# The pool layer of a two-block network: seven-product projections, the residual through DRAM, and norms by half rows

## The chip, the cores and the metric

The kernel runs on one core of one Trainium2 chip. The metric is the device time of one execution in microseconds (us). Names used below: PE is TensorE (matmuls; PEld its weight loads), DVE is VectorE, ACT is ScalarE, POOL is GpSimd, SP is SyncE, which here only issues DMAs.

## What is computed

Two networks run one after the other on 1024 rows of 1024 features, in 32-bit floats. The first has two layers: windowed attention, then the pool layer that this case is about, then a norm. The second has one block (neighbourhood attention, a gated recurrence, a mix w_o, an MLP). Cut to the part that matters:

```python
def pool_layer(h, w_in, w_mix, scale, w_out):
    u, z = jnp.split(h @ w_in, [POOL_WIDTH], axis=-1)          # 1024 -> 2 x 1024
    p = multiscale_pool(u)                                     # windows 2, 4, 8, 16; one per group of 256
    m = jnp.einsum('bsgc,gcd->bsgd', p, w_mix).reshape(B, S, POOL_WIDTH) * scale
    return (m * jax.nn.silu(z)) @ w_out

x = x + attn_layer(rmsnorm(x, norm_g[0]), ...)
x = x + pool_layer(rmsnorm(x, norm_g[1]), ...)
x = rmsnorm(x, final_g)                                        # end of the first network
a = rms_norm(h, norm_mix)                                      # start of the second
```

`multiscale_pool` takes for each group the mean over the last 2, 4, 8 or 16 rows, less the row itself.

## The kernel before

**Precision.** Every operand of a large product is split into a high part (a rounded copy, made by ACT) and a low part (the difference, made by DVE or POOL). `mm3` issues three matmuls for each 128x128 by 128x512 term: high x high, low x high, high x low (lines 108, 110, 111). `split_w` (L79, L80) and `split_evac` (L118, L119) make the parts. Weights go through three buffers each for the raw tile (`wraw`) and its parts (`whi`, `wlo`).

**Order.** The program is written in order of the data; a scheduler places each engine's instructions by that order and by its own estimate of when inputs are ready. `issue_after(i)` keeps the instructions of a block behind instruction i on i's engine. All waits are made automatically, by the tile that is read or overwritten. A pool's memory can be taken again when the tiles that lay there are done with.

**End of attention.** The residual X of 8 row tiles sits in SBUF. The output projection runs over four pairs of k blocks (kp), each over two column halves and eight row tiles, and adds each bank to X (`out_piece`, L281). Four row tiles are normed (`norms`, into copies), turned by PE into the feature-major operand `xx` (`transposed`, L175 to L178), the other four after the first weights of the pool layer have run.

**Pool layer.** It loops over four groups g. In each, two column blocks of u are projected over both row halves (`pieces_fm`, evacuated by ACT at L620), pooled by DVE (window sums L632, difference L639, parts L118 and L119), then two blocks of z with SiLU (L653), then the mix product (evacuated at L662 with scale and z), and the result m times the group's 256 rows of w_out is added to X (`add_out`, L539). So the output projection is spread over the groups. In group 3 it runs in two row halves: behind each row tile a hook squares X (L683), multiplies by final_g (L686, six row tiles on POOL, two on DVE), stores the product to `d_h` and squares again; `group` forms the two norms of four row tiles at once, the scaled copies are turned (`feature_major`), and the first pieces of two gate projections (`gate0`, `gate1`) fill PE meanwhile.

**Where the other scheme is already used.** The second block computes three products by seven half-size products instead of eight (Strassen's scheme in Winograd's form): with the row halves and the k (or column) halves as 2x2 blocks, sums S1 to S4 of the blocks of the operand and sums of the weight blocks are made, and seven products are added into banks. For w_o this is a sequence of `times` over four banks each (L1391), with `split_a`, `split_b` and `less` (L1375, weight differences) between; for the up projection it is `first_two`, `sums` (L1634 to L1648) and `pair`, which handles two column blocks at a time: weight sums (`weight_sums`, by `vec`, L1595), products A11, A12, S2, S1, S3, S4, A22 of 12 matmuls each, evacuations by ACT (L1540) and adds by DVE (L1544); for the down projection blocks are stored to DRAM (`d_u`) and read back through a ring of three buffers, the residual through `d_x` (adds at L1791).

Of the kernel before, what the change touches and what calls it, by code (L numbers as in the profile page):

```python
# [30 lines left out]
def fused_kernel(tc, a, out, stop=None, dbg=None):  # L31
# [180 lines left out]

    x = a["x"][0]
# [17 lines left out]
    w_in = a["attn_w_in"][0]  # L231
    w_out = a["attn_w_out"][0]
    def norm_into_xt(gcol, alloc, pool, xtag="xn", xbufs=5):

        xx = XT()

        def norms(half):
            xn = []
            for i, n in ((0, 4),) if half == 0 else ((0, 2), (2, 2)):
                ss = small.tile([P, n], F32, name="nm" if n == 2 else "ss4")  # L240
                for j in range(n):
                    junk = pool.tile([P, 1024], BF16, name="junk", bufs=1)
                    nc.scalar.activation(out=junk, in_=X[:, half * 4 + i + j, :], func=AF.Square,
                                         accum_out=ss[:, j:j + 1])
                r = rsqrt(ss, D)
                for j in range(n):
                    xr = pool.tile([P, D], F32, name=xtag, bufs=xbufs)
                    if j % 2:
                        nc.scalar.activation(out=xr, in_=X[:, half * 4 + i + j, :], func=AF.Copy, scale=r[:, j:j + 1])
                    else:  # L250
                        nc.vector.tensor_scalar_mul(xr, X[:, half * 4 + i + j, :], r[:, j:j + 1])
                    xn.append(xr)
            return xn

        def do(half, xn=None):
            transposed(alloc, xn or norms(half), gcol, xx, half * 4)
        return xx, norms, do

# [24 lines left out]
    with lay:  # L283
# [213 lines left out]
        xpool = xp.enter_context(tc.tile_pool(name="xpool", bufs=1, side="right"))  # L497
        X = xpool.tile([P, NT, D], F32, name="X")
        up2 = xp.enter_context(tc.tile_pool(name="up2", bufs=1, side="right"))
        pst = xp.enter_context(tc.tile_pool(name="pst", bufs=4, space=PSUM))  # L500
        psm = xp.enter_context(tc.tile_pool(name="psm", bufs=4, space=PSUM))
        for t in range(NT):
            if t < 4:
                nc.gpsimd.tensor_copy(out=X[:, t, :512], in_=x0[:, t, :])
                nc.scalar.dma_start(out=X[:, t, 512:], in_=x[t * P:(t + 1) * P, 512:])
            else:
                nc.scalar.dma_start(out=X[:, t, :], in_=x[t * P:(t + 1) * P, :])
# [3 lines left out]
        xx, norms, norm_half = norm_into_xt(g_pool, lambda k: pst.tile([P, 512], F32, name="tp"), up2, "pp", 6)  # L511
        for kp in range(4):
            ws = {}
            if kp == 3:
                ws = {ch: out_weights(kp, ch) for ch in range(2)}
                wu0 = w_cols(a["pool_w_in"][0], 0)
            for ch, t in ([(ch, t) for ch in range(2) for t in range(NT)] if kp < 3 else
                          [(ch, t) for t in range(NT) for ch in range(2)]):
                if ch not in ws:
                    ws[ch] = ws0[kp] if kp < 2 and ch == 0 else out_weights(kp, ch)  # L520
                if kp >= 2 or ch or t >= 4:
                    out_piece(psm, kp, ws[ch], X[:, t, ch * 512:ch * 512 + 512], t)
                if kp == 3 and (ch, t) == (1, 5):
                    xn = norms(0)
                if kp == 3 and (ch, t) == (1, 6):
                    norm_half(0, xn)
    dump("x1", X)
# [4 lines left out]
    def add_out(ps_pool, terms, ws_by_ch, hook=None, scale=None, tiles=range(NT), half=None, by_ch=False):  # L532

        for t, ch in [(t, ch) for ch in range(2) for t in tiles] if by_ch else [(t, ch) for t in tiles for ch in range(2)]:
            csl = slice(ch * 512, ch * 512 + 512)
            ps = ps_pool.tile([P, 512], F32, name="mm")
            mm3(ps, list(zip(terms(t), ws_by_ch[ch])))
            if scale is None:
                nc.vector.tensor_tensor(out=X[:, t, csl], in0=X[:, t, csl], in1=ps, op=ALU.add)  # L539
            else:  # L540
                nc.vector.scalar_tensor_tensor(out=X[:, t, csl], in0=X[:, t, csl], scalar=scale[:, t:t + 1],
                                               in1=ps, op0=ALU.mult, op1=ALU.add)
            if half:
                half(t, ch)
            if hook and ch:
                hook(t)

    w2 = a["w_in_2"][0]
    dram = ctx.enter_context(tc.tile_pool(name="dram", bufs=1, space=bass.MemoryType.DRAM))
# [25 lines left out]
    with ExitStack() as ph:  # L575
# [35 lines left out]
        for g in range(4):  # L611
# [59 lines left out]
            if g < 3:  # L671
                add_out(psm, terms, mixed((0, 1)))
# [675 lines left out]
    def turned(half, k):  # L1348
# [3 lines left out]
        return ps  # L1352

# [510 lines left out]
```

## Time and profile before

| | us |
|---|---|
| median of 3 runs | 2377.55 (2375.57 to 2377.82) |
| profiled execution | 2379.98 |
| its span, first to last instruction | 2378.2 |
| PE busy | 2309.6 |
| DVE, ACT, POOL busy | 1426.5, 971.5, 791.5 |

The granted TensorE clock is 0.992 of full speed in the mean. Times inside the span count from its first instruction. The pool layer lies from about 461 to 780 us, the w_o product of the second block from 1636 to 1730, its up projection from 1730 to 2050, its down projection from there to the end.

### The profile page before, as it was taken

The page shows a single profiled execution, that of the slowest core. Times are in us where ns is not written, and L with a number is a line of the kernel's source. Part 1 is how long each engine was busy: PE and PEld are TensorE (multiplying, and loading weights), DVE is VectorE, ACT ScalarE, POOL GpSimd, SP SyncE. Part 2 cuts the span into 40 slices and gives each one's busy share as a digit, 9 for nine tenths or more (in the row PEclk, how much of TensorE's full clock was granted, in tenths as well). Part 3 has the DMA queues.
Part 4 walks back from the last instruction along what each step waited for, and adds up shares of the span by engine and source line. Part 5 has one row for each costly group of instructions (what it writes and reads, how often), then busy time and mean ns, then how long its engine had stood idle before and what let it go on. Part 6 is the DMA issues. An engine that isn't in the chain of part 4 may idle for free. (4 is left out here: it accounts for less than half of the span.)

```text
span 2378.2 us, 32052 instructions
## 1 busy us (share of the span) xinstructions
PE 2309.6 (97%) x12054; PEld 1921.4 (81%) x12054; DVE 1426.5 (60%) x2602; ACT 971.5 (41%) x1808; POOL 791.5 (33%) x528
## 2 busy tenths in 40 slices
PE   7999999999999999999999999999989999999997
PEld 6877777888887888878988888877768888878886
DVE  5566677654367255553265746759784444786775
ACT  5344452422226454543232232423555555533334
POOL 2112123112226343431212112126354444444455
PEclk9999999999999999999999999999999999999999
DMA  5111103111124222211111111467235444754331
GB/s 160 36 28 36 28 27 108 40 45 58 40 63 138 62 68 67 54 58 45 46 52 54 41 54 54 139 200 258 71 120 199 146 151 164 267 220 168 107 124 71
DMA packets 237147, 230.01 MB, mean 97 GB/s; under 512 B 59896, under 2 KB 179022, under 8 KB 233408
## 3 DMA queue, kind: packets, MB, share of 16 engines
q1 hardware_dynamic: 228176, 210.31, 27.5%
q10 hardware_dynamic: 8224, 16.00, 1.8%
q0 software_dynamic: 592, 1.65, 0.3%
q8 instruction: 95, 1.56, 0.3%
q14 instruction: 60, 0.49, 0.1%
HBM read 168.68 MB, written 59.24 MB: 96 GB/s over the span
## 5 line engine op out<-in xcount | busy, mean ns | idle before, releaser
L108 PE MATMUL mm<-xh,whi 128*128 128x512 f32 (+2 forms) x1744 | 670.9, 385 | 8.5 <-DVE st L1544 3.7
L110 PE MATMUL mm<-xl,whi 128*128 128x512 f32 (+2 forms) x1744 | 665.3, 382 | 0.0
L111 PE MATMUL mm<-xh,wlo 128*128 128x512 f32 (+2 forms) x1744 | 662.3, 380 | 2.3 <-POOL wlo L80 2.2
L80 POOL TENSOR_TENSOR wlo<-wraw,whi 128x1024 fp32r<-128x1024 f32 (+1 forms) x127 | 300.2, 2369 | 894.3 <-ACT whi L79 838.4
L108 PEld LDWEIGHTS mm<-xh,whi 128*128 128x128 f32 x1744 | 329.2, 189 | 70.2 <-issue 3.5
L111 PEld LDWEIGHTS mm<-xh,wlo 128*128 128x128 f32 x1744 | 329.3, 189 | 66.1 <-POOL wlo L80 3.4
L110 PEld LDWEIGHTS mm<-xl,whi 128*128 128x128 f32 x1744 | 329.4, 189 | 56.2
L79 ACT CAST whi<-wraw 128x1024 fp32r<-128x1024 f32 (+1 forms) x127 | 128.9, 1018 | 371.8 <-PE mm L110 174.3
L111 PE MATMUL mm<-whi,xl 128*128 128x512 f32 (+1 forms) x688 | 247.8, 360 | 0.0
L110 PE MATMUL mm<-wlo,xh 128*128 128x512 f32 (+1 forms) x528 | 184.6, 350 | 3.3 <-POOL wlo L119 2.6
L108 PE MATMUL mm<-whi,xh 128*128 128x512 f32 (+1 forms) x528 | 184.7, 350 | 2.1 <-DVE X L281 1.3
L111 PEld LDWEIGHTS mm<-whi,xl 128*128 128x128 f32 x688 | 130.7, 190 | 19.3
L108 PE MATMUL mm<-whi,xl 128*128 128x512 f32 x352 | 138.5, 394 | 4.7 <-ACT whi L118 2.4
L110 PE MATMUL mm<-wlo,xl 128*128 128x512 f32 x352 | 138.8, 394 | 3.9 <-POOL wlo L119 3.9
L1668 POOL TENSOR_TENSOR wlo<-raw,whi 128x1024 fp32r<-128x1024 f32 (+1 forms) x42 | 84.1, 2003 | 100.8 <-ACT whi L1667 100.8
L110 PEld LDWEIGHTS mm<-wlo,xh 128*128 128x128 f32 x528 | 99.8, 189 | 17.2 <-POOL wlo L119 3.9
L108 PEld LDWEIGHTS mm<-whi,xh 128*128 128x128 f32 x528 | 99.8, 189 | 15.4 <-DVE X L281 1.7
L119 POOL TENSOR_TENSOR wlo<-wraw,whi 128x1024 fp32r<-128x1024 f32 x30 | 80.6, 2692 | 80.4 <-ACT whi L118 78.0
L1595 DVE TENSOR_TENSOR st<-st 128x512 f32<-128x512 f32 x64 | 61.1, 975 | 57.8 <-ACT st L1581 56.8
L1791 DVE TENSOR_TENSOR X<-X,mm 128x512 f32<-128x512 f32 x112 | 73.1, 680 | 37.2 <-PE mm L111 37.2
L878 DVE CUSTOM_DVE_ANT_0 s<-S,bi 128x400 f32<-128x400 f32 x64 | 34.5, 571 | 94.6 <-PE S L870 94.6
L119 DVE TENSOR_TENSOR pl<-PT,ph 100x512 fp32r<-100x512 f32 (+2 forms) x128 | 83.6, 668 | 10.3 <-ACT ph L118 9.3
(370 smaller groups left out, 4400.1 us busy)
## 6 DMA issues: line engine op xcount, KB each, us to landing
wraw<-in_w_in_dram SPq DMA_DIRECT2D x48, 512.0 KB, 3.8
d_S<-st SPq DMA_DIRECT2D x64, 256.0 KB, 4.7
raw<-in_w_up_dram SPq DMA_DIRECT2D x30, 512.0 KB, 5.0
d_A<-st ACTq DMA_DIRECT2D x48, 256.0 KB, 2.0
fa<-d_S SPq DMA_DIRECT2D x10, 1024.0 KB, 4.9
wraw<-in_pool_w_in_dram SPq DMA_DIRECT2D x18, 512.0 KB, 3.9
fa<-d_A SPq DMA_DIRECT2D x9, 1024.0 KB, 4.8
wraw<-in_attn_w_in_dram SPq DMA_DIRECT2D x32, 256.0 KB, 3.2
```

The lines of the kernel that those rows point to most:

```text
L79: nc.scalar.copy(out=hv[:, i:i + n], in_=view[:, i:i + n])
L80: nc.gpsimd.tensor_tensor(out=lv[:, i:i + n], in0=view[:, i:i + n], in1=f(hv[:, i:i + n]), op=ALU.subtract)
L108: nc.tensor.matmul(ps, lhsT=lh[0], rhs=rh[0], start=first and i == 0, stop=False, skip_group_check=chain)
L110: nc.tensor.matmul(ps, lhsT=lh[0], rhs=rh[1], start=False, stop=False, skip_group_check=chain)
L111: nc.tensor.matmul(ps, lhsT=lh[1], rhs=rh[0], start=False, stop=last and i == n - 1, skip_group_check=chain)
L119: return (lo_eng or nc.vector).tensor_tensor(out=lo, in0=src, in1=f(hi), op=ALU.subtract)
L878: nc.vector.tensor_tensor_reduce(out=s, in0=sps[j], in1=bs[j], scale=-0.125, scalar=-NEG, op0=ALU.add, op1=ALU.min, accum_out=mx)
L1595: return nc.vector.tensor_tensor(out=out_, in0=x_, in1=y_, op=op)
L1668: nc.gpsimd.tensor_tensor(out=lv, in0=view, in1=f(hv), op=ALU.subtract)
L1791: added[:] = [nc.vector.tensor_tensor(out=dst, in0=dst, in1=banks[t], op=ALU.add)]
```

## The change

- **General functions.** What the second block used for the seven-product scheme (`bank`, `vec`, `load_d`, `load_w11`, `less`, `split_into`, `split_b`, `times`, `banks4`, the weight sums, `first_two`, `sums`, `pair`) is moved ahead of both blocks; `project_pairs` holds the loop over pairs of column blocks, with a `res` object for what is done with each result. The second block calls the same code with the same order of work. `Rows` holds row tiles, squares them by halves and scales them in place.
- **End of attention.** Kp 0 and 1 run as before; kp 2 and 3 run per row half h, so that their weights are loaded and split twice. Each row tile is squared by halves, stored to DRAM (`d_x1`) and then scaled in place; rows 0 to 3 are turned while rows 4 to 7 are still being produced.
- **Input projection** by `project_pairs`, 8 pairs; even pairs are two blocks of u, odd pairs two of z. `Pooled` copies and adds the banks, applies SiLU for odd pairs, and pools a group behind each even pair. Group g is mixed in pair 2g+2, and group 3 after the last pair. No group is projected out there: m and its sums S1 to S4 go to DRAM (`d_m`), 28 stores of 256 KB.
- **Output projection** afterwards, as seven products of 48 matmuls, over all of K. A11 and A12 are read back for groups 0 to 2 (group 3's part is made from SBUF), then S2, S1, A22, S4, S3 through a ring of three 1 MB buffers. The residual is read back from `d_x1`, and the three other weight blocks are loaded there.
- **Norms of the second block** by half rows: `add_p` adds, squares, multiplies by final_g on DVE, squares; `second_norms` runs for rows 0 to 3, 4 to 6 and 7, and scales in place. Rows 0 to 3 are turned during the last two products, rows 4 to 7 after the first pieces of `gate0` and `gate1`; the weights of `gate1` are split behind the last scaling. The loads of meta tokens and of the position bias (rpb) move from the start of the pool layer to here.

Core of the diff:

```diff
+        for h in range(2):
+            for ch in range(2):
+                ws = out_weights(2, ch)
+                for t in range(4 * h, 4 * h + 4):
+                    out_piece(psm, 2, ws, X.at(t, ch), t)
+            ws = [out_weights(3, ch) for ch in range(2)]
+            if h:
+                with tc.issue_after(scaled[0]):
+                    wu0 = w_cols(w_pin, 0)
+            for i in range(4):
+                t = 4 * h + i
+                for ch in range(2):
+                    out_piece(psm, 3, ws[ch], X.at(t, ch), t)
+                    X.squares(t, ch)
+                nc.sync.dma_start(out=d_x1[t], in_=X.x[t])
+                if t == 3:
+                    scaled = X.norms(0, 4)
+                if t == 6:
+                    X.norms(4, 3)
+                for k in ((0, 1, 2), (3, 4, 5), (6, 7), ())[i] if h else ():
+                    turn_half(xx, X.x, g_pool, k, a11)
+        scaled = X.norms(7, 1)
...
+            def last(self, p, ps):
...
+                if p % 2 == 0:
+                    self.pp[p // 2] = {j: self.pooled(p // 2, j) for j in (1, 0)}
...
+        project_pairs(w_pin, lambda p, i: (p % 2) * 1024 + (p // 2 * 2 + i) * P, 8, xx, sh, g_pool, X.x, a11,
+                      lambda j: stage(), stage, raw_tile, opened, pooled, wu0, scaled[0])
+
+        w11 = load_w11(wv)
+        oa = [xt.tile([P, KT, 512], F32R, name=n) for n in ("xh0", "xl0")]
...
+        mix(3)
+        ops = split_b(w11)
+    xp.close()
...
+        load_d(w21, wv, 1, 0)
+        load_d(w22, wv, 1, 1)
+        load_d(w12, wv, 0, 1)
...
+        load_m("S2")
+        for t in range(NT):
+            nc.sync.dma_start(out=X.x[t], in_=d_x1[t])
+            if t == 3:
+                load_m("S1")
+        load_m("A22")
...
+                vec(dst, dst, banks[i], ALU.add)
+                if done:
+                    square(t, ch, 0)
+                    vec(dst, dst, fg[:, ch * 512:ch * 512 + 512], ALU.mult)
+                    square(t, ch, 1)
...
+        B, A_ = banks4(), banks4()
+        times(B, oa[0], ops, True)
+        ops = split_b(w21)
+        o6 = split_a("xl1", in_two(ring["S2"]))
+        load_m("S4")
+        o4 = split_a("xh1", in_two(ring["A22"]))
+        load_m("S3")
+        with tc.issue_after(made[0].ins):
+            less(w12, w12, w22)
+        add_p(B, 0, 0)
+        times(A_, oa[1], ops, True)
...
+        zp = ph.enter_context(tc.tile_pool(name="zp", bufs=2))
+        scaled = second_norms(7, 1)
+        gate0 = gate(psm, zp, 0, w=wg)
+        gate0[0]()
+        with tc.issue_after(scaled[0]):
+            wg = w_cols(w2, 4096 + P)
+        gate1 = gate(psm, zp, 1, w=wg)
+        gate1[0]()
```

Removed are `norm_into_xt`, `add_out`, `mixed`, `group`, `feature_major` and the loop over groups around them.

More of the change, by code (lines that the diff above doesn't have):

```diff
@@ L228, in fused_kernel @@
     lm = const.tile([P, 2, 4], F32, name="lm")
[L231 to L257, printed above, removed]
+    w_in, w_out = a["attn_w_in"][0], a["attn_w_out"][0]
+    w_pin, w_mix, w_pout = a["pool_w_in"][0], a["pool_w_mix"][0], a["pool_w_out"][0]
+    dram = ctx.enter_context(tc.tile_pool(name="dram", bufs=1, space=bass.MemoryType.DRAM))
+    d_x1 = dram.tile([NT, P, D], F32, name="d_x1")
+    d_m = {n: dram.tile([P, 4, 512], F32, name=f"d_m{n}") for n in ("A11", "A12", "A22", "S1", "S2", "S3", "S4")}
     def split_ot(cs, hfs, eng):
@@ new lines, in fused_kernel @@
+        times(B, oa[0], ops, True)
[8 more added lines that the diff above has]
+        times(A_, oa[1], ops, True)
+        with tc.issue_after(made[0].ins):
+            less(w11, w11, w12)
+        ops = o6, split_b(w11)
+        o5 = split_a("xh0", in_two(ring["S1"]))
@@ L741, in fused_kernel @@
         gate0[1]()
         gate1[1]()
-        with tc.issue_after(last[3].ins):
+        with tc.issue_after(scaled[0]):
             wk0_ = w_cols(w2, 512)
-    xp.close()
+        last = scaled
     xx = x2
@@ L1515, in fused_kernel @@
         add_x(C, 0, 1, False, True)
-        scaled = norms(0, 4)
+        scaled = X.norms(0, 4)
         with tc.issue_after(scaled[0]):
```

823 lines of the change are left out of this document (439 added, 384 removed).

## The prediction

> **What bounds the kernel now.** The first view is the page's busy time and its chain.
>
> ```profile
> span 2378.2 us, 32052 instructions
> PE 2309.6 (97%) x12054; PEld 1921.4 (81%) x12054; DVE 1426.5 (60%) x2602; ACT 971.5 (41%) x1808; POOL 791.5 (33%) x528
> PE 22%; DVE 2%; issue 1%; ACT 1%; DMA 0%; POOL 0%; SPq 0%; DVEq 0%; ACTq 0%
> ```
>
> PE is busy for 97% of the span, and what the chain keeps is almost all PE. So time follows the number of matmuls, plus the moments in which PE has none to issue. Both are read from busy time by stretch. The columns are us, then busy us (instructions) of PE, PEld, DVE, ACT, POOL, then granted clock, DMA share, GB/s.
>
> ```profile
> 385.00:461.00 76.00, 75.71 (x346) 62.20 (x347) 48.67 (x97) 21.65 (x32) 18.50 (x15) 1.00 0.26 63
> 461.00:712.00 251.00, 250.93 (x1111) 205.37 (x1110) 125.05 (x152) 63.91 (x87) 60.54 (x33) 1.00 0.17 51
> 712.00:792.00 80.00, 73.87 (x349) 59.21 (x348) 53.75 (x92) 48.62 (x76) 40.32 (x24) 0.98 0.40 132
> 1636.00:1730.00 94.00, 85.23 (x371) 68.44 (x370) 75.29 (x79) 42.57 (x67) 49.50 (x22) 0.96 0.31 115
> 1730.00:1795.00 65.00, 55.68 (x238) 43.49 (x236) 55.72 (x76) 37.37 (x61) 35.95 (x19) 0.95 0.41 133
> 1795.00:2047.00 252.00, 251.52 (x1102) 206.82 (x1102) 111.66 (x146) 138.44 (x203) 111.20 (x53) 1.00 0.48 163
> 2047.00:2124.00 77.00, 75.34 (x330) 61.49 (x329) 65.13 (x53) 31.85 (x36) 39.66 (x14) 1.00 0.83 305
> ```
>
> The first three rows are the end of the attention output projection, the pool layer, and its last group with the norms behind it, up to the first two gate projections. The other four are stages that already use the seven-product scheme: the w_o product of the second block (1636), the start of its up projection (1730), that projection in steady state (1795), the first quarter of its down projection (2047). They are the price list for this change. I call lost what PE is not busy, and the stretch times one minus the clock. That is 0.3 + 0.1 + (6.1 + 1.6) = 8.1 us for the pool stretch now; 8.8 + 3.8 = 12.6 for w_o; 9.3 + 3.3 = 12.6 for the start of the up projection; 0.5 in its steady state; 1.7 at the down projection.
>
> **The matmuls.** The input projection now takes 16 column blocks x 8 k x 2 halves x 3 = 768 matmuls of 128x512; in the new scheme it takes 8 pairs x 7 products x 4 k x 3 = 672. The output projection takes 8 row tiles x 2 halves x 8 k x 3 = 384, then 7 x 48 = 336. Mix, gates and transposes keep their number. 144 matmuls go. The steady-state row gives one as 252 / 1102 = 0.2287 us, and PE is full in the 461 row, so they are on the path: 144 x 0.2287 = 32.9 us off. The edits below give some of it back.
>
> **Entry into the input projection.** Four weights of attention's output are loaded and split again (kp 2 and 3 run per row half). The rows are squared, stored (eight 512 KB stores on SP's queue, with the later weight loads behind them) and scaled in place, and the second row half is turned while `sums` makes S1 to S4 from it. Attention's extra splits cost nothing: POOL is busy 18.5 of 76 us there, and four more splits are four of the rows below on ACT and POOL. If that cover is gone, one costs 1.0 + 2.4 us. The store of the last row is waited for by its scaling, as it is at 1730 today, where it hides behind the first two products. The rest is the code that runs at 1730 today, and PE's waits there are these.
>
> ```profile
> PE mm L108 <- DVE xl L1634: 3.3, 2, 2.2
> PE mm L108 <- DVE st L1544: 2.9, 2, 1.9
> PE mm L1351 <- DVE xl L1634: 1.7, 1, 1.7
> ```
>
> ```profile
> L79 ACT CAST whi<-wraw 128x1024 fp32r<-128x1024 f32 (+1 forms) x127 | 128.9, 1018 | 371.8 <-PE mm L110 174.3
> L80 POOL TENSOR_TENSOR wlo<-wraw,whi 128x1024 fp32r<-128x1024 f32 (+1 forms) x127 | 300.2, 2369 | 894.3 <-ACT whi L79 838.4
> ```
>
> PE waits for DVE (55.7 of 65 us busy there), which must make the sums of four column pairs. The new entry has the same instructions, so I take 12.6 us. Bounds: 0.1 (today's 461 row) and 12.6 plus one more pooled burst, 10 us (next part).
>
> The granted clock falls with such waits.
>
> ```profile
> 1756.00:1761.00 5.00, 5.00 (x15) 3.97 (x16) 5.00 (x5) 3.33 (x6) 4.57 (x2) 0.66 0.03 8
> ```
>
> Here it is 0.66 behind a longest wait of 2.2 us. The Trainium skill, page "TensorE: Matmul & The Clock Gate", section "Why this matters for your kernels", asks only for no idle gap above about 3 us between bursts. By that rule the 3.3 us of clock would not be lost and the sum below would be 3.3 us lower; the trace disagrees (0.66 after 2.2 us), and the measurement decides.
>
> **The pairs.** Per pair DVE gets four weight sums and three adds, ACT four copies (or SiLU), POOL about 2.5 splits. Two pairs bring one pooled group: up to four window sums, a difference and a low part for each of two tiles, in one go behind an even pair.
>
> ```profile
> L632 DVE TENSOR_TENSOR sum<-u 128x1039 f32<-128x1039 f32 x8 | 19.3, 2418 | 43.3 <-ACT u L620 43.3
> L632 DVE TENSOR_TENSOR sum<-sum 128x1037 f32<-128x1037 f32 (+2 forms) x12 | 15.8, 1317 | 0.4
> L639 DVE SCALAR_TENSOR_TENSOR u<-sum,u 128x1008 f32<-128x1008 f32 x8 | 9.6, 1200 | 0.0
> L119 DVE TENSOR_TENSOR pp<-u,pp 128x1024 fp32r<-128x1024 f32 x8 | 9.8, 1225 | 9.4 <-ACT pp L118 9.4
> L1595 DVE TENSOR_TENSOR st<-st 128x512 f32<-128x512 f32 x64 | 61.1, 975 | 57.8 <-ACT st L1581 56.8
> L662 DVE SCALAR_TENSOR_TENSOR z<-mm,vecs,z 128x512 f32<-128x512 f32 x16 | 12.0, 750 | 48.7 <-ACT z L653 30.2 <-PE mm L111 16.9 <-ACT mh L118 1.4
> ```
>
> The largest burst is 2 x (2.4 + 3 x 1.3 + 1.2 + 1.2) = 17.5 us. A pair lasts 84 x 0.2287 = 19.2 us and DVE has about 8 us of other work in it (111.7 x 19.2 / 252 = 8.5 in the steady row), so two pairs with their mix (38.4 + 24 x 0.2287 = 43.9 us of PE) hold 17.5 + 16 + mix 7 (4 x 0.75 + 4 x 0.98) = 41 us at the widest window, less at the others. It fits, but the weight sums of the next pair can come late. The steady row's 0.5 us in 252 (111.7 us of DVE) is the low bound. The high bound is the overhang of three bursts, about 10. I take 2, nearest the steady row, since its pairs also end in four sums of 0.98. The mix blocks go out by 28 stores of 256 KB on SP; the DMA share is 0.17 in the 461 row, so they are free there.
>
> **Output projection.** It replaces the adds of each group and gets first blocks of m from DRAM, mix 3 in between, then S2, S1, A22, S4, S3 through a ring of three, the residual and the weights. Two stages give bounds: 1.7 us at the down projection, which also reads its blocks back from DRAM with DVE busy for 65 of 77 us, and 12.6 at w_o. Mean: 7.2. Two things here are worse than in both. DVE multiplies 16 half rows by final_g, which is now six full rows on POOL and two on DVE. And S2 can only be formed after mix 3, then stored, read and split.
>
> ```profile
> L686 POOL TENSOR_TENSOR X<-X,u 128x1024 f32<-128x1024 f32 x6 | 14.4, 2429 | 6.1 <-ACT sum L683 6.1
> ```
>
> ```profile
> d_S<-st SPq DMA_DIRECT2D x64, 256.0 KB, 4.7
> ub<-d_S SPq DMA_DIRECT2D x6, 1024.0 KB, 6.0
> ```
>
> From the last mix matmul: three sums of 1.0, store 4.7, load 6.0, two splits of 1.0 + 1.2 makes 18 us; PE has half of the first product and all of the second, 72 x 0.2287 = 16.5 us. So 2 us more: 9.2, call it 9. It can go below (1.7), and up to the 26 of the third rival.
>
> **The end.** After the last add the chain is square 0.8, product 1.0, square 0.8, some sixteen small instructions of about 0.2, scaling 0.7: 7 us from rows of the kind of L1595 and the ones below. PE has one gate piece meanwhile (24 x 0.2287 = 5.5 us), since the second gate's weights are split only after the scaling. With DVE's backlog of two or three instructions (2 us) and the eight low parts of 0.74 behind the transposes I take 6 us. Bounds: 2.5 (the two waits now) and 10 (no cover).
>
> ```profile
> PE tp L175 <- DVE pp L721: 1.4, 1, 1.4
> PE tp L175 <- DVE xl L178: 1.1, 1, 1.1
> ```
>
> ```profile
> L1744 ACT ACTIVATE junk<-X x16: 612/631/632, 2306.4 to 2370.7; 128x512 bf16<-128x512 f32 x16
> ```
>
> ```profile
> L178 DVE SCALAR_TENSOR_TENSOR xl<-tp,vecs,xh 128x512 fp32r<-128x512 f32 x32 | 21.7, 743 | 3.9 <-ACT xh L177 3.9
> ```
>
> The rpb and meta loads on POOL's queue move from the start of the pool layer into the output projection: six issues, hidden by POOL's idle half there; if not, one delays a split by its issue.
>
> **Sum.** Lost after: 12.6 + 2 + 9 + 6 = 29.6 us, against 8.1 now: 21.5 given back of 32.9, so 11.4 us faster. The profiled execution took 2379.98 us (span 2378.2 and 1.8 around it), 2.4 above the median of 2377.55. So 2368.6 against its own time, 2366 as a median.
>
> **Rivals.** A difference under 0.2% (4.8 us) I count as none.
>
> 1. Quiet transitions. The input for the products is there in time as at 2047, and the entry is shorter because DVE has no add backlog from a product before it. Lost: entry 8, pairs 0.5, output 4, end 4, together 16.5; 24.5 us faster, 2353. For it speaks the 1.7 us at 2047, against it that DVE was 55.7 of 65 us busy with the very same sums.
>
> 2. DVE becomes the bound of the output projection. Its 75.3 us at w_o plus 16 products of 0.98, mix 3 (7), the m blocks' low parts and the meta norm (7), less the 4.5 of two block differences, is about 101 us over 85.2 + 5.5 = 90.7 us of PE, and the low parts stretch when POOL splits at the same time:
>
> ```profile
> L119 DVE TENSOR_TENSOR xh<-a,xh 128x1024 fp32r<-128x1024 f32 x4 | 11.3, 2863 | 0.0
> ```
>
> against 1225 ns for the same shape above. With half of w_o's 19 us of DVE idle left, the stage loses 101 + 9 - 91 = 19 us, not 9: 1.4 us faster in all, 2376, no change. The Trainium skill, page "SBUF — State Buffer", section "Who interferes with whom", says that a VectorE instruction with two SBUF inputs and a GpSimd instruction that reads SBUF exclude each other for the whole instruction. By that rule this rival is the one to expect wherever both queues are full; the trace agrees on the mechanism (2863 against 1225 ns), but at 2047, with 39.7 us of POOL beside 65.1 of DVE, PE lost only 1.7 us.
>
> 3. The output projection starves (the other side). Its SBUF pool opens where the pool layer's pools close, so residual, weights and blocks can be loaded only as pair 7 and mix 3 let go: weights 3.1 MB, S2, S1, A22 3.1, residual 4.2, m blocks and stores 2.2 is 12.6 MB. At the 305 GB/s of the 2047 row that is 41 us, while PE has 24 + 96 matmuls, 27.5 us, before it needs S2 and the sums with w12. If all of it is queued ahead of these, the third product waits 14 us with 3 us of split behind, and the reused ring makes the later products wait for about as much as at w_o (9): 26 us lost, 5.6 us slower, 2383. It decides from 25.2 us lost in that stage (9 + 11.4 + 4.8). For it: PE's cover is known and short. Against: the order asks for the weights first.
>
> That the matmuls do not become fewer is no rival: the count follows from the loops.
>
> **How the numbers follow.** Forecast 0.42 (own range 2357 to 2373), quiet transitions 0.20 (2347 to 2357), DVE-bound 0.20 (2373 to 2382), starved 0.18 (2382 up). Faster is 0.42 + 0.20, same 0.20, slower 0.18. The range 2349 to 2386 cuts a small part of the first rival and half of the third.
>
> **What would show it.** PE's matmul count falls by 144, and the pairs take 19.2 us each. At the entry PE waits for DVE's fused sums (the line that is L1634 now) for 8 to 10 us, with one or two half-clock stretches. Between pairs PE waits under 0.5 us a pair; if weight sums stand in PE's waits there, the pairs' term is wrong. In the output projection, waits behind a DMA landing or a DVE weight difference speak for rival 3, waits for low parts with DVE over 90% busy for rival 2, under 4 us of waits for rival 1. The prediction is wrong as a whole if the stage after 792 starts later by itself, or if the pool stretch is not 11 us shorter.

## The result, and the profile after

The changed kernel takes 2415.06 us (median of 4 runs, 2414.16 to 2417.35) against 2377.69 before on the same chip: ratio 1.0157 [1.014, 1.0175], 1.6% slower where 0.5% faster was forecast. The profiled execution took 2414.16. Page of the changed kernel, span and busy time:

```profile
span 2412.4 us, 32252 instructions
PE 2285.8 (95%) x11910; PEld 1899.6 (79%) x11910; DVE 1501.5 (62%) x2699; ACT 1018.3 (42%) x1911; POOL 851.9 (35%) x559
```

PE has the 144 matmuls less and is busy for 23.8 us less, yet the span is 34.2 us longer. The first score matmul of the stage behind the pool stretch starts at 858.6 us, before at 825.6, so nearly all of it (33.1) is lost in the pool stretch. Busy time by stretch, columns as in the prediction (us, then PE, PEld, DVE, ACT, POOL, clock, DMA share, GB/s): entry, pairs, output projection in two parts, end.

```profile
461.00:530.00 69.00, 57.33 (x244) 45.15 (x243) 63.34 (x87) 35.52 (x56) 39.74 (x24) 0.93 0.26 74
530.00:674.00 144.00, 132.79 (x560) 106.62 (x558) 102.57 (x108) 51.67 (x73) 64.18 (x32) 0.98 0.31 95
674.00:735.00 61.00, 31.55 (x119) 24.68 (x120) 36.30 (x39) 19.78 (x27) 18.72 (x13) 0.78 0.72 255
735.00:790.00 55.00, 55.00 (x263) 45.32 (x262) 42.16 (x65) 31.07 (x67) 17.19 (x7) 1.00 0.23 82
790.00:824.00 34.00, 27.25 (x127) 21.89 (x126) 16.27 (x61) 15.35 (x26) 8.76 (x13) 0.90 0.31 101
```

By the prediction's measure (not busy, plus the stretch times one minus the clock):

| stretch | lost, predicted | lost, measured |
|---|---|---|
| entry | 12.6 | 11.7 + 4.8 = 16.5 |
| pairs | 2 | 11.2 + 2.9 = 14.1 |
| output projection | 9 | 61 - 119 x 0.2287 = 33.8 |
| end | 6 | 6.8 + 3.4 = 10.2 |

In the third row half of the stretch is idle, and half clock counts only where PE works, so there the loss is the time less that of its 119 matmuls. With 0.8 us ahead of the entry (76 less 75.24 busy, 385 to 461 us) that is 75.4; less the 8.1 of before and the 32.9 of the matmuls it makes 34.4 us slower. The sum closes; the four terms of loss were too small.

PE's waits, the longest of each stretch in the same order (total us, times, longest):

```profile
PE mm L108 <- DVE u L226: 4.7, 1, 4.7
PE mm L282 <- DVE xl L386: 3.0, 1, 3.0
...
PE mm L108 <- ACT z L843: 7.4, 3, 3.3
PE mm L108 <- DVE z L226: 3.0, 2, 2.6
...
PE mm L108 <- ACT whi L118: 17.0, 1, 17.0
PE mm L110 <- POOL wlo L119: 11.3, 2, 8.1
...
PE mm L108 <- ACT whi L79: 5.2, 1, 5.2
```

**Output projection.** The names are those of the last links only. Ahead of the loads, SP's own wait and the DMA view, 670 to 735 us:

```profile
SPq L908 <- DVE z L226: 12.5, 3, 11.8
```

```profile
GB/s 0 0 0 314 338 222 334 376 395 403 402 279 422 401 418 414 396 274 211 215 265 294 342 396 413 429 403 418 424 323 55 0 0 0 0 0 0 0 0 0
DMA packets 4785, 15.56 MB, mean 239 GB/s; under 512 B 544, under 2 KB 574, under 8 KB 4144
X<-d_x SPq DMA_DIRECT2D x8, 512.0 KB, 18.4
```

The store of mix 3's first sum stands on SP until DVE has made it (11.8 us, to 674.3), and behind it every load of the stage; they start only at 677.4. (Group 3 has five stores to `d_m`, the groups before it seven each: the trace has 26 in all, not the 28 of the change and the prediction.) Then 15.6 MB run at 211 to 429 GB/s until about 720 us; a row of the residual lands 18.4 us after its issue (median). POOL and DVE, 685 to 700 us, in order of time (start, us, then the instruction; in brackets the idle time before it and what ended it):

```profile
690.29 0.57 POOL L957 TENSOR_SCALAR rp<-rp 120x127 f32<-120x127 f32 x1 [5.41 <-DMA rp<-in_na_rpb_dram]
690.92 1.87 POOL L962 DMA_DIRECT2D d_rpb<-rp  x2
692.69 4.80 POOL L119 TENSOR_TENSOR wlo<-w,whi 128x1024 fp32r<-128x1024 f32 x2
```

```profile
691.04 0.14 DVE L141 TENSOR_SCALAR hx<-ss 16x1 f32<-16x1 f32 x1 [14.05 <-ACT mjunk L150]
691.39 6.12 DVE L128 SCALAR_TENSOR_TENSOR w<-r,hx 16x1 f32<-16x1 f32 x1
697.73 0.21 DVE L128 SCALAR_TENSOR_TENSOR w<-r,hx 16x1 f32<-16x1 f32 x1
```

POOL waits for the 14.5 KB of rpb to land, with the low parts that the second product needs behind it: 8.1 us of PE. DVE stands idle for 14.05 us too: next in its order is the meta norm, whose tokens land at 689.8. And an instruction on 16x1 elements takes 6.12 us on DVE where its twin takes 0.21: it ends when POOL's second split ends. The third product then waits 17.0 us: its weights are the difference w11 - (w12 - w22), which the code holds behind the split of A22, and A22's load stands behind all eight rows of the residual.

**Pairs.** In the odd pairs ACT's copy for the S3 product stands behind the high part of a pooled tile, and that one waits for DVE's window sums. DVE's rows, 461 to 674 us (L226 is the helper that all sums and adds go through):

```profile
L226 DVE TENSOR_TENSOR sum<-sum 128x1037 f32<-128x1037 f32 x6 | 15.8, 2638 | 0.1
L226 DVE TENSOR_TENSOR raw<-raw,wraw 128x512 f32<-128x512 f32 x7 | 9.1, 1305 | 0.0
L226 DVE TENSOR_TENSOR raw<-raw 128x512 f32<-128x512 f32 x7 | 9.0, 1292 | 0.0
L226 DVE TENSOR_TENSOR wraw<-raw 128x512 f32<-128x512 f32 x7 | 4.8, 690 | 0.3
```

The same kind of 128x512 instruction takes 690 ns in one group and 1292 in another, and a window sum has a mean of 2638 ns. Counted one by one in the trace, the 34 of these 128x512 instructions (f32, both inputs in SBUF) that had no POOL split or sum beside them took 674 to 694 ns, the 15 others 1589 in the mean; those with one input in PSUM took 680 and 681. POOL in the same window:

```profile
L276 POOL TENSOR_TENSOR wlo<-raw,whi 128x1024 fp32r<-128x1024 f32 x11 | 29.7, 2701 | 23.1 <-ACT whi L275 23.0
```

**End.** The weights of `gate1` are split behind the last scaling, and PE has run out of `gate0` by then: 5.2 us, and half clock behind it.

### The profile page after: what moved, and what is told of

The parts are those of the page before. It is cut to its first block, busy times and chain, and to the rows that moved or that the text cites. A ratio compares the mean times of both kernels' runs of the same rounds, so it can differ in the third digit from the quotient of the medians.

```text
span 2412.4 us, 32252 instructions
## 1 busy us (share of the span) xinstructions
PE 2285.8 (95%) x11910; PEld 1899.6 (79%) x11910; DVE 1501.5 (62%) x2699; ACT 1018.3 (42%) x1911; POOL 851.9 (35%) x559
## 5 line engine op out<-in xcount | busy, mean ns | idle before, releaser
L108 PE MATMUL mm<-xh,whi 128*128 128x512 f32 (+2 forms) x1616 | 623.8, 386 | 27.3 <-ACT whi L79 6.8
L111 PE MATMUL mm<-xh,wlo 128*128 128x512 f32 (+2 forms) x1616 | 614.2, 380 | 2.9 <-POOL wlo L80 2.9
L110 PE MATMUL mm<-xl,whi 128*128 128x512 f32 (+2 forms) x1616 | 616.7, 382 | 0.0
L80 POOL TENSOR_TENSOR wlo<-wraw,whi 128x1024 fp32r<-128x1024 f32 (+1 forms) x107 | 250.2, 2344 | 749.8 <-ACT whi L79 691.0
L111 PE MATMUL mm<-whi,xl 128*128 128x512 f32 (+1 forms) x752 | 273.1, 363 | 0.0
L110 PE MATMUL mm<-wlo,xl 128*128 128x512 f32 x416 | 165.2, 397 | 20.1 <-POOL wlo L119 20.1
L108 PE MATMUL mm<-whi,xl 128*128 128x512 f32 x416 | 163.8, 396 | 18.6 <-ACT whi L118 18.2
L276 POOL TENSOR_TENSOR wlo<-raw,whi 128x1024 fp32r<-128x1024 f32 (+1 forms) x60 | 124.9, 2083 | 144.4 <-ACT whi L275 144.3
L111 PEld LDWEIGHTS mm<-whi,xl 128*128 128x128 f32 x752 | 143.3, 191 | 21.9
L110 PEld LDWEIGHTS mm<-wlo,xl 128*128 128x128 f32 x416 | 79.5, 191 | 39.1 <-POOL wlo L119 22.8
L108 PEld LDWEIGHTS mm<-whi,xl 128*128 128x128 f32 x416 | 79.2, 191 | 37.0 <-ACT whi L118 19.2
L226 DVE TENSOR_TENSOR st<-st 128x512 f32<-128x512 f32 x64 | 63.3, 1010 | 57.8 <-ACT st L1852 56.7
```

The costliest lines, as they stand in the source:

```text
L80: nc.gpsimd.tensor_tensor(out=lv[:, i:i + n], in0=view[:, i:i + n], in1=f(hv[:, i:i + n]), op=ALU.subtract)
L108: nc.tensor.matmul(ps, lhsT=lh[0], rhs=rh[0], start=first and i == 0, stop=False, skip_group_check=chain)
L110: nc.tensor.matmul(ps, lhsT=lh[0], rhs=rh[1], start=False, stop=False, skip_group_check=chain)
L111: nc.tensor.matmul(ps, lhsT=lh[1], rhs=rh[0], start=False, stop=last and i == n - 1, skip_group_check=chain)
L226: return nc.vector.tensor_tensor(out=out_, in0=x_, in1=y_, op=op)
L276: nc.gpsimd.tensor_tensor(out=lv, in0=view, in1=f(hv), op=ALU.subtract)
```

## The experiments

The theories that the expectations name: A, engines and queues that take their instructions in order hold what stands behind a waiting one; B, the parts add up; C, DVE is full, so what leaves one place on it comes back at another; D, the bytes of the output projection at some 400 GB/s set it, whatever the order; E, DVE and POOL shut each other out. The runs were made in four sets, on three chips, and each is compared with the kernel before beside it, whose median lay between 2377.4 and 2379.2 us. Across sets the ratios are what counts; one ratio is known to 0.1 to 0.2%, or 2 to 5 us.

### One queue at a time

e1_rpb: the lines that load rpb, scale it and store it to `d_rpb` move from the output projection to the start of the pool layer.

> The position-bias chain (load, scale on POOL, three stores) is moved from the output projection back to the start of the pool layer. Theory A (the second product waits for POOL, which stands in its queue behind the landing of the 14.5 KB rpb load; the third waits for weight differences that are queued behind the split of A22, the last block to be loaded): the 8.1 us wait of PE for the low part of w21 goes to under 2 us, but the third product's start is set by another chain, so the gain is small, 1 to 4 us (the 1 MB of bias traffic also leaves the crowded stretch): about 2412. Theory B (the waits are independent and add up): 8 to 10 us faster than the changed kernel, about 2406. Rival C (DVE is the bound of the output projection): no change, 2415.

e2_diffs: the weight differences no longer wait for A22's split, which comes after the fourth product; the load of S3 moves behind the split of S1.

```diff
-        o4 = split_a("xh1", in_two(ring["A22"]))
-        load_m("S3")
-        with tc.issue_after(made[0].ins):
-            less(w12, w12, w22)
+        less(w12, w12, w22)
...
-        with tc.issue_after(made[0].ins):
-            less(w11, w11, w12)
+        less(w11, w11, w12)
...
+        load_m("S3")
...
         ops = split_a("xl0", in_two(ring["S4"])), split_b(w22)
+        o4 = split_a("xh1", in_two(ring["A22"]))
```

> The weight differences are no longer queued behind the split of A22; A22 is split after the fourth product is issued. Theory A: the 17.4 us wait before the third product falls to about 5 us (weights w12 and S2 are the next late things), 10 to 14 us faster than the changed kernel, 2401 to 2405. Rival C (DVE bound): under 3 us. Rival D (the stretch is bound by 15 MB at about 400 GB/s, whatever the order): under 4 us, since the same bytes must land first.

e3_stores: group 3's five stores to `d_m` are issued by ACT in place of SP.

> Only the five stores of the last mix go out by ACT's queue, so that the weight loads behind them on SP start when their memory is free (about 664 us into the span instead of 677). Theory A: loads land about 10 us earlier, the third product starts 6 to 10 us earlier, 2405 to 2409. Rival D: the same, since bytes start earlier. Rival C (DVE bound): no change. If w21, w22 and w12 are held by memory that is not free before the stores have been read, the gain is under 3 us.

e4_three: all three.

> The three edits together. Theory A: the output projection loses 8 to 12 us instead of 34, so 22 to 26 us faster than the changed kernel, 2389 to 2393. Theory B: the sum of the three single gains. Rival D: no more than 12 us, 2403. Rival C: no change.

| | us | ratio to before |
|---|---|---|
| e1_rpb | 2409.64 | 1.0132 [1.0116, 1.0147] |
| e2_diffs | 2410.4 | 1.013 [1.0115, 1.0145] |
| e3_stores | 2413.92 | 1.0143 [1.0126, 1.016] |
| e4_three | 2402.49 | 1.0099 [1.0084, 1.0115] |

Of 33.8 us lost in that stage, taking three causes away brought 5.4, 4.7 and 1.1 us by the medians, and together 12.6. So the parts add up (theory B: 11.2), theory A's 22 to 26 us are missed, and theory D's bound (at most 12) holds within the noise as well. In e1 the second product's wait of 8.1 us is gone, as theory A had it, and the third product's rose from 17.0 to 20.4. In e3 SP issues the first weight load at 667.4, but two of its weight loads then wait 15.2 us until stores of m have landed, so their memory was not free before. That is the condition under which less than 3 us were expected. In e2, and in e4, the third product waits for something else:

```profile
PE mm L108 <- DVE X L226: 22.3, 1, 22.3
```

```profile
PE mm L108 <- DVE X L226: 12.4, 1, 12.4
```

The third product writes into banks that must first be added to the residual. In e4 rows 0 to 3 of the residual land between 695 and 699 us, but DVE adds the first at 710.8: ahead of it stand the meta norm, which waits until 693.8 for the meta tokens, six instructions of weight differences and the split of S2.

### DVE's order, the gate, the entry, earlier loads

Each on top of the one before. e5_end starts from e4_three; its two edits lie far apart, so each is read in its own stretch:

```diff
-                split_evac(p_h, p_l, pr)
+                nc.vector.tensor_copy(out=p_h, in_=pr)
+                vec(p_l, pr, f(p_h), ALU.subtract)
...
-        with tc.issue_after(scaled[0]):
-            wg = w_cols(w2, 4096 + P)
+        wg = w_cols(w2, 4096 + P)
```

> On top of the three edits together (2402.5 us): the high part of the pooled tiles is copied by DVE in place of ACT, and the weights of gate1 are split without being held behind the last scaling of rows 0 to 3. Theory A (engines that wait in order hold what stands behind them): the three waits of 3.2 to 3.7 us at the S3 product of the odd pairs (ACT's z copy stands behind a pooled copy that waits for DVE) go, with the half-clock stretches behind them, and so does the 5.4 us gap before gate1 at the end; DVE gets eight copies of about 0.6 to 1.2 us. 11 to 15 us less: 2388 to 2391. Theory C (DVE has no room there): the wait comes back as one for DVE's adds or weight sums in the same pairs and only the gate's 6 to 7 us are gained: 2395 to 2397.

e6_order, with `last` the instruction that ends what the third product needs (the lines that these replace are left out):

```diff
+        last = less(w11, w11, w12)
+        with tc.issue_after(last.ins):
+            add_p(B, 0, 0)
+            o6 = split_a("xl1", in_two(ring["S2"]))
...
+        last = made[0].ins
...
-        less(w21, w21, w11)
-        less(w11, w22, w11)
-        add_p(A_, 0, 0, True)
+        with tc.issue_after(last):
+            less(w21, w21, w11)
+            less(w11, w22, w11)
+        with tc.issue_after(last):
+            add_p(A_, 0, 0, True)
```

and the same around the meta norm.

> On top of e5_end: DVE's order in the output projection is written out. Before the third product only what it needs: two weight differences, the four residual adds, the low parts of S2; the other two differences, the adds of the second bank set and the meta norm (whose load lands at 694 us and holds DVE until 697) come behind them. Theory A: the 12.8 us gap before the third product shrinks to 3 to 6 us, 7 to 9 us less than e5_end. Theory D (the bytes at some 420 GB/s set it: the residual lands at 695 to 699 whatever DVE does): at most 3 us less. Theory C (DVE's amount of work sets it): the gap moves to the fourth or fifth product, within 2 us of e5_end.

e7_all, in `pair`:

```diff
-            if p + 1 >= NF:
+            if p + 1 >= NF or (p == 0 and w is w_pin):
                 ready[p + 1] = added[0].ins
```

> On top of e6_order, at the entry of the pairs: the weight sums of pair 1 stay behind DVE's first add of pair 0, as they do in the later pairs. In the trace so far these sums (four instructions, two of them stretched to 2.8 us beside POOL's splits) stand ahead of the two adds, and PE waits 4.7 us for the adds. Theory A: that wait goes, and its half clock, while pair 1's first weights come 1 to 2 us later: 3 to 6 us less than e6_order. Theory C: DVE is full there, the wait moves to pair 1's S2 product: within 2 us of e6_order, either side.

e8_early moves the line that allocates w21, w22 and w12 ahead of the one for X, and `load_m("S2")` from ahead of the residual's loads to behind row 3.

> On top of e7_all: the three weight blocks take the first places of the memory that the output projection opens, the residual rows the places behind, and S2 is loaded behind rows 0 to 3, so that no load before S2 stands behind the last m stores (they land at 684 us). Theory A (what is late is late by its queue): weights and residual are issued from about 668 to 680 in place of 679 to 689, land 5 to 10 us sooner, and the third product waits less than 2 us: 3 to 6 us less than e7_all. Theory D says the same sign but no more than the bytes brought forward allow (4 MB at 420 GB/s, 10 us). If the memory comes free no earlier: no change.

| | us | ratio to before |
|---|---|---|
| e5_end | 2396.53 | 1.0075 [1.0058, 1.0092] |
| e6_order | 2394.25 | 1.0066 [1.0051, 1.0081] |
| e7_all | 2394.95 | 1.0068 [1.0053, 1.0083] |
| e8_early | 2388.07 | 1.004 [1.0025, 1.0055] |

e5: the gate's wait is gone. But with the pooled copy on DVE, PE's waits in the pairs come to 14.2 us (530 to 680 us), where the changed kernel has 10.4:

```profile
PE mm L108 <- DVE z L226: 9.2, 3, 4.6
PE mm L108 <- ACT z L852: 5.0, 2, 2.9
```

The time, 6.0 us less, is what theory C gave for the gate alone. e6: the wait of 12.5 us before the third product is gone, as theory A has it; smaller waits at this and the later products (0.9, 1.1, 1.7, 2.1 and 4.1 us) took back most, and the median fell by 2.3 us, not 7 to 9. That fits theory D (at most 3) and is near C's bound of 2; this run does not tell them apart. e7: nothing. The wait at the entry moved from pair 0's adds to pair 1's (e6, then e7, 461 to 530 us):

```profile
PE mm L108 <- DVE u L226: 4.7, 1, 4.7
```

```profile
PE mm L108 <- DVE z L226: 6.0, 2, 5.0
```

e8: 6.9 us less. The residual lands 8.2 us after its issue (median; 11.4 in e7) and the waits of the stage fall below 2 us each: 8.1 us together, where the changed kernel has 30.2. DVE has the same work as in e7, so its amount was not what made these waits. Loads that come sooner do help; a kernel with fewer bytes was not run, so how much of the rest was theory D stays open.

### Which engine makes the low parts

e9_nohi is e8_early with the pooled copies on ACT again.

> e8_early with the pooled copies back on ACT, all else as it is. In e5_end PE's waits in the pairs came to 5.0, 2.5, 2.6, 3.3 and 2.7 us (behind DVE's adds), against 1.7, 3.0, 3.7 and 3.2 us with ACT. Theory C for that edit (DVE has no room, the copies only made its burst longer): 3 to 5 us less than e8_early, 2383 to 2385. Theory A (ACT's order was the cause there, the copies help): 3 to 6 us more.

e10_spread moves the parts of one pooled tile behind the first add of the odd pair, and the whole pooling of the other tile behind the second (`parts` is the split that ended `pooled`):

```diff
+                if p % 2 and key == "22":
+                    self.pp[p // 2] = {1: self.parts(self.w)}
+                if p % 2 and key == "12":
+                    self.pp[p // 2][0] = self.parts(self.pooled(p // 2, 0))
...
-                    self.pp[p // 2] = {j: self.pooled(p // 2, j) for j in (1, 0)}
+                    self.w = self.pooled(p // 2, 1)
```

> e9_nohi with each group's pooling spread over its odd pair: the window sums of one tile behind the even pair as now, its high and low part behind the odd pair's first add, the other tile's window sums and parts behind the odd pair's second add. The work is the same. Theory A (a burst of pooling stands in DVE's and ACT's queues ahead of the adds and copies that PE waits for): the waits at the S3 and A22 products of the odd pairs (about 3 us each, with 1.7 us of half clock) go: 8 to 12 us less than e9_nohi, 2372 to 2377. Theory C (it is the amount of DVE's work in these pairs): the waits move to the mix or to the next pair's weight sums: within 2 us.

e11_port, with `low` read by `split_w` and `split_group` in place of `nc.gpsimd`:

```diff
+        low[0] = nc.vector
         project_pairs(w_pin, ...
+        low[0] = nc.gpsimd
```

> e10_spread with the low parts of the pool layer's input weights made by DVE in place of POOL (24 of 1024 columns and some halves). In the trace so far a DVE instruction of 1.2 us takes 2.7 to 3.3 us where POOL splits at the same time, and 0.7 becomes 1.7. Theory E (the two engines shut each other out, so POOL's 2.4 us cost DVE more than the 1.2 us the same work takes on DVE): DVE's pairs get shorter, the entry above all (63 of 69 us busy now, two waits of 3.4 and 5.4 us): 4 to 10 us less than e10_spread. Theory C (DVE's own work sets it; 24 instructions of 1.2 us more): 5 to 15 us more. The Trainium skill, page 'SBUF — State Buffer', section 'Who interferes with whom', says that the pair exclude each other for the whole instruction; by that rule theory E is the one to expect.

| | us | ratio to before |
|---|---|---|
| e9_nohi | 2381.77 | 1.001 [1.0, 1.0019] |
| e10_spread | 2383.52 | 1.0013 [1.0004, 1.0023] |
| e11_port | 2367.37 | 0.9946 [0.9931, 0.996] |

e9 gains 6 us, so e5's copies were a loss: the cause was not ACT's order but the length of DVE's burst. e10: the same work at other moments moves the waits and gains nothing; theory A missed its 8 to 12 us. e11 gains 16 us at one stroke, more than the 4 to 10 of theory E. So it is neither this order of DVE's work nor its own amount (it got more of it), but what POOL does to it.

### The same edit alone, and further

e12_port_alone is the changed kernel with that edit and no other; e13_best is e11_port without the spreading; e14_out extends the edit to mix 3 and to the output projection's first four products; e15_up extends it to the second block's up projection.

> The changed kernel with one edit alone: the low parts of the pool layer's input weights are made by DVE in place of POOL. Theory E (DVE and POOL shut each other out, and that is what made the entry and the pairs lose 16.5 and 14.1 us): the waits at the entry and in the pairs fall as they did on top of the other edits, 13 to 19 us less than the changed kernel, 2396 to 2402. Rival F (that gain needed the other edits: without them DVE's added work stands ahead of the adds of the first pairs): less than 6 us gained, above 2409.

> e11_port without the spreading of the pooling over the odd pair, which by itself gave nothing. Theory E: within 2 us of e11_port (2367.4), since with POOL quiet a burst of pooling is 8 us shorter and fits. Theory A for the bursts (spreading matters once DVE also makes the low parts): 3 to 6 us slower than e11_port.

> e13_best with the low parts of the weights of mix 3, of w11, w21 and of the third and fourth product's weights made by DVE too. Theory E taken further (every low part is cheaper on DVE while DVE's instructions are stretched beside it): 1 to 4 us less. Theory C (at the first products DVE is busy 53 to 55 of 61 us, so ten more instructions of 1.2 us stand ahead of what PE waits for): 2 to 8 us more.

> e13_best with the low parts of the second block's up projection made by DVE too (that projection is not part of this change and is alike in both kernels). It takes 39 splits of 2.4 us off POOL, which there also stretch DVE's sums (995 against 690 ns), but PE loses only 0.5 us of 252 in its steady part and 3 to 13 at its start. Theory E: 2 to 6 us less than e13_best, all of it at the start. Theory C (about 39 x 1.2 us more on DVE, 120 of 252 us busy now, is no bound but stands ahead of the adds): 0 to 5 us more.

| | us | ratio to before |
|---|---|---|
| e12_port_alone | 2398.28 | 1.0087 [1.0065, 1.0109] |
| e13_best | 2366.24 | 0.995 [0.9934, 0.9965] |
| e14_out | 2371.35 | 0.9971 [0.9959, 0.9983] |
| e15_up | 2368.21 | 0.9954 [0.9937, 0.997] |

e12, entry and pairs by stretch, and DVE's rows there:

```profile
461.00:530.00 69.00, 61.76 (x268) 49.20 (x267) 65.83 (x103) 38.29 (x59) 15.74 (x13) 0.95 0.27 76
530.00:671.00 141.00, 136.89 (x589) 111.12 (x587) 106.09 (x133) 51.83 (x71) 12.38 (x13) 0.99 0.39 125
```

```profile
L277 DVE TENSOR_TENSOR wlo<-raw,whi 128x1024 fp32r<-128x1024 f32 x11 | 13.5, 1223 | 5.1 <-ACT whi L276 5.0
L277 DVE TENSOR_TENSOR wlo<-wraw,whi 128x1024 fp32r<-128x1024 f32 x9 | 11.0, 1222 | 2.3 <-ACT whi L276 2.2
L227 DVE TENSOR_TENSOR sum<-sum 128x1037 f32<-128x1037 f32 x6 | 7.4, 1231 | 0.0
```

A low part costs 1.22 us on DVE and 2.70 on POOL. DVE took over 24.5 us of them in these rows alone, and its busy time in the two stretches rose from 165.9 to 171.9: the rest of its work shrank by at least 18.5 us (more in truth, since the second row now reaches some 12 us into the output projection), the window sums of 128x1037 from 2638 to 1231 ns. PE lost 7.2 + 3.5 + 4.1 + 1.4 = 16.2 us there, against 30.6. By the medians the kernel is 0.7% (some 17 us, with an uncertainty of about 7) faster for it, at the middle of what theory E gave; rival F falls. The profiled execution is the slowest of its four (2406.13, median 2398.28) and shows less: the first score matmul starts 12.8 us sooner than in the changed kernel, and code that is alike in both then takes 4.6 us more. It is not that the low parts come sooner: in these stretches of the changed kernel PE waited for ACT's copies and DVE's results and for no low part of a weight. So this cause is shown, on the changed kernel itself, for most of the pairs' loss and for 5.8 of the entry's 16.5 us; the output projection's waits stay (8.7, 16.6 and 3.3 us).

e13 confirms that spreading is not needed: its ratio is e11's within the noise, 0.5% faster than before and 2% faster than the change as made. Its profiled execution is the slowest of its four runs (span 2368.7). e14 is 5 us worse, within what theory C gave: PE now waits 1.8 + 1.8 us at the third product and 3.2 at the fifth, where e13 waits 0 and 0.7 (12.8 us in all from 655 to 740 us, 8.5 in e13). DVE is not fuller for it (49.6 of 60 us busy, 52.7 in e13), so it is the place of the added low parts in its order that fits, which no run tests by itself. The low parts belong on DVE where its two-input instructions are what PE waits for; that this pays elsewhere is not a rule. e15 shows no gain: between 1760 and 2010 us of its trace PE is busy for 250.0 of 250 us against 245.6 in e13, all of it from the start of the up projection (from 1790 on both have 250.0), but the medians do not tell the two apart.

## Why the prediction was wrong

The gain was right and the loss against it was not: 75.4 us lost where 29.6 were forecast. Of the 45.8 us between, 24.8 lie in the output projection and 12.1 in the pairs.

- **The matmuls** (-32.9 us): right, count and price.
- **Entry** (12.6): 16.5. The mechanism, waits for DVE's sums and adds, was named; it was mis-sized by 4. Weight sums of pair 1, stretched to as much as 2.9 us beside POOL, stood ahead of pair 0's adds, but that order was not the cause: e7 put them behind the first add, and the wait moved. The part that is POOL's is shown by e12 (10.7 left).
- **Pairs** (2, bounds 0.5 to 10): 14.1, outside its bounds. The failed step is the 41 us at the widest window in 43.9 us of PE: "It fits, but the weight sums of the next pair can come late." The amount does fit: DVE is busy for 102.6 of 144 us. But the burst was priced too low, and what waits behind it are the odd pair's copies on ACT (7.4 us of PE) and adds on DVE (3.0). Added up from its instructions, the widest burst took 20.6 us of DVE instead of 17.5, the two before it 18.2 and 15.6, where the same prices give 14.8 and 12.2; with the low parts on DVE (e12) they take 18.0, 12.9 and 10.5, and PE's waits in the stretch fall from 10.4 to 4.1. The warning stood in the quoted rows of before: a first window sum of 128x1039 had a mean of 2418 ns, the next sums 1317. The first is a stretched instruction (all eight had a POOL split beside them). In the new pairs all six sums of 128x1037 had one. The steady rows of the up projection could not price this: DVE's sums are stretched there too (995 ns), but nothing in its queue is a burst; that this is why they cost nothing there was not tested.
- **Output projection** (9, bounds 1.7 to 26): 33.8. This step failed most. Three statements in it were wrong. That the stores are free at a DMA share of 0.17 is right for the bytes, but the last group's stores held the loads: first by SP's order, until 674.3, and, with the stores on ACT (e3), by the memory that they still read; so e3 alone brought 1.1 us. That the rpb and meta loads are "hidden by POOL's idle half" is wrong, since POOL waits for the landing and holds the low parts: 8.1 us of PE, of which e1 brought 5.4; the meta norm held DVE for 14 us as well, and what that cost by itself no run shows. And two splits behind the load of S2 were taken as the end of the chain, while the weight differences stood behind A22's split: 17.0 us, of which e2 brought 4.7. These three brought 12.6 us together, order (e6) and earlier loads (e8) some 2 and 7 more; what is left in e8, 8.1 us of waits, is of the size that was forecast.
- **End** (6, bounds 2.5 to 10): 10.2. The mechanism was named: one gate piece covers 5.5 us, and the second gate's weights are split behind the scaling. PE is idle for 6.8 us, near the 6; the term put at nothing was the half clock behind it, 3.4.
- **Rivals.** The third (starvation, slower, decided from 25.2 us lost in the stage) came true with 33.8, at a chance of 0.18 and with too low a price. Its mechanism was there, since loads waited for memory and stood in one queue. That its 14 + 3 us for the third product are just the 17.0 measured is luck: it counted 12.6 MB at 305 GB/s, the trace has 15.6 MB at 211 to 429, and the last link was the order of A22's split. The second was given for the output projection, where DVE was busy for 36.3 of 61 us: false there. Its mechanism decided the pairs and a third of the entry's loss, where the prediction had not looked for it. The Trainium skill, page "SBUF — State Buffer", section "Who interferes with whom", says that a VectorE instruction with two SBUF inputs contends with a GpSimd instruction that reads SBUF. The traces agree: 2638 against 1231 ns for the same instruction with and without POOL's splits beside it. The down projection's 1.7 us of loss was no evidence against that rule in another stage.
- **The clock.** Half clock came behind waits as forecast; it is 4.8 us of the entry's loss, 2.9 of the pairs' and 3.4 of the end's.

## What to carry to other kernels

When work moves to an engine that has room on average, ask what its instructions do to those of its neighbour: look in the trace for one form of instruction with two durations, and price the new stage with the longer one. For each queue that is filled in order, find the item whose input comes last and count everything behind it, loads included. And when several things are late together, the wait that goes is partly taken up by the next: in e2 waits of 28 us went, one of 22 us came in their place, and the kernel gained 4.7. Go on until no long wait is left in the stage, and price each cause by the time, not by the wait that bore its name.

## What was not expected of the hardware

- A DVE instruction on 16x1 elements took 6.12 us in place of 0.21. It began while POOL issued two DMAs (1.87 us) and ended with the second of two POOL splits of 2.4 us that ran back to back: it did not get its turn between them.
- Low parts of 128x1024 take 1.22 us on DVE and 2.70 on POOL, and POOL's own time is also that of waiting: counted between 461 and 674 us of the changed kernel, the ten without a DVE instruction of two SBUF inputs beside them took 2.40 us in the mean, the fourteen others 2.95.
- In the changed kernel, from 461 to 830 us, the granted clock fell to half with each wait of PE from 2.8 us up and with none up to 2.65, in stretches of 3.41 us or multiples of it (the longest 20.48: 0.78 in the mean over 674 to 735 us). That is no threshold: in e13 one such stretch came behind two waits of 1.7 and 1.9 us, 2.4 us apart.
